# Two rows per partition, and a cut last group, in an average pool over windows of 16

## Chip, core and metric

One core of one Trainium2 chip runs the kernel; the other cores are idle. The metric is the device time of one execution in microseconds (us). The profile's span is 1.7 to 2.2 us shorter than that time in the runs here. All runs were single-core runs with a granted clock of 1.0, agreeing within 0.3%. A ratio below is the mean time of one kernel's runs over that of the other's runs of the same rounds, so it is not quite the ratio of the medians that stand beside it.

## The reference

The input is 32 x 256 rows of 4096 float32. Every row is cut into 256 windows of 16 neighbours, and the output is the mean of each window.

```python
x = np.random.randn(32, 256, 4096).astype(np.float32)     # 134 MB in
for i in range(256):
    result[:, :, i] = np.mean(x[:, :, 16 * i : 16 * (i + 1)], axis=-1)   # 8.4 MB out
```

There is one addition per loaded number, so the kernel is a stream: load, sum, scale, store.

## The kernel before

The 8192 rows go in 64 blocks of 128, one row to a partition. SyncE issues a 2 MB load, VectorE sums each window, ScalarE multiplies by 1/16, and ScalarE's queue issues a 128 KB store.

```python
xpool = ctx.enter_context(tc.tile_pool(name="xpool", bufs=8))
opool = ctx.enter_context(tc.tile_pool(name="opool", bufs=8))
for i in range(ntiles):                      # 64
    r0 = i * P
    x_tile = xpool.tile([P, length], mybir.dt.float32)
    nc.sync.dma_start(out=x_tile, in_=x_flat[r0 : r0 + P, :])
    o_tile = opool.tile([P, output_size], mybir.dt.float32)
    nc.vector.reduce_sum(out=o_tile,
        in_=x_tile.rearrange("p (o w) -> p o w", w=window), axis=mybir.AxisListType.X)
    nc.scalar.mul(out=o_tile, in_=o_tile, mul=inv_w)
    nc.scalar.dma_start(out=out_flat[r0 : r0 + P, :], in_=o_tile)
```

## Time and profile before

| | before |
|---|---|
| time, median | 345.66 us (345.62 to 345.74, 4 runs) |
| span of the profiled run | 343.8 us |
| VectorE busy | 282.9 us, 82% |
| bytes moved, mean rate | 142.65 MB, 415 GB/s |
| last load packet ends (DMA packet records) | 335.84 us |
| from there to the end of the span | 8.0 us |

These are lines of the page of the kernel before: VectorE's (DVE) share, the span in 40 slices (DMA is the mean busy share of the 16 DMA engines in tenths), the DMA queues (q1 carries the loads, q10 the stores), the group of reduces, and the DMA issues with the median time from issue to landing.

```profile
DVE 282.9 (82%) x64; ACT 28.0 (8%) x65; POOL 0.2 (0%) x4
...
DMA  8999999999999999999999999999999999999991
GB/s 305 427 423 435 432 427 423 425 434 431 427 421 424 437 428 425 425 424 439 428 423 425 427 435 425 427 423 431 434 427 423 423 429 435 427 425 422 434 419 39
DMA packets 18436, 142.65 MB, mean 415 GB/s; under 512 B 2048, under 2 KB 10240, under 8 KB 10240
...
q1 hardware_dynamic: 9216, 134.22, 91.4%
q10 hardware_dynamic: 9216, 8.39, 7.0%
...
L47 DVE TENSOR_REDUCE o_tile<-x_tile 128x256 f32<-128x4096 f32 x64 | 282.9, 4420 | 57.9 <-DMA x_tile<-in_x_dram 57.9
...
x_tile<-in_x_dram SPq DMA_DIRECT2D x64, 2048.0 KB, 20.8
out_dram<-o_tile ACTq DMA_DIRECT2D x64, 128.0 KB, 10.1
```

The DMA row is full from the second slice to the second-last, and VectorE's idle time is all spent waiting for loads: the DMA engines are the limit. VectorE is not far behind, though: 4.42 us of work for each block, against about 5.2 us between landings.

The end of the chain that ended last (start us, duration us, what):

```profile
315.45 20.77 DMA x_tile<-in_x_dram
...
336.35 4.43 DVE o_tile L47
340.78 0.02 issue
340.80 0.42 ACT o_tile L52
```

The last block's reduce, multiply and store come after all loading is done. That tail of 8 us has the DMA engines nearly idle (mean busy share 0.10 to 0.11 from 336 us on).

The trace also has a record of each DMA packet. Sorted by size, the median durations in both kernels (the rows from 2 KB on in the second column are from the changed kernel) are:

```
 4 B semaphore write    9 ns     2 KB store packet    84 ns
 1 KB store packet     46 ns    16 KB load packet    611 ns
 352 B store packet    21 ns    32 KB load packet   1213 ns
```

They fit 8.4 ns per packet plus 0.0368 ns per byte.

### The profile page before, as it was taken

What the parts mean: (1) busy time and instruction counts of PE and PEld (TensorE: products, weight loads), DVE (VectorE), ACT (ScalarE), POOL (GpSimd) and SP (SyncE); (2) the same over time, 40 slices, a digit from 0 to 9 for tenths busy, and PEclk for the clock granted to TensorE, in tenths of its full rate; (3) what the DMA queues carried; (4) which work ended last, traced back from release to release, by engine and by line L of the source; (5) the groups of instructions that cost most, each with busy time, mean ns of one, the idle gap of its engine ahead of it and who ended that gap; (6) DMA issues with size and microseconds to landing.
All of it is one profiled execution on the core that took longest, in us unless ns stands there. A gap on an engine that the chain in (4) does not pass through costs nothing.

```text
span 343.8 us, 475 instructions
## 1 busy us (share of the span) xinstructions
DVE 282.9 (82%) x64; ACT 28.0 (8%) x65; POOL 0.2 (0%) x4
## 2 busy tenths in 40 slices
DVE  0988988988888889889888888888888888898895
ACT  1000000000000000000000000000000000000000
POOL 0000000000000000000000000000000000000000
DMA  8999999999999999999999999999999999999991
GB/s 305 427 423 435 432 427 423 425 434 431 427 421 424 437 428 425 425 424 439 428 423 425 427 435 425 427 423 431 434 427 423 423 429 435 427 425 422 434 419 39
DMA packets 18436, 142.65 MB, mean 415 GB/s; under 512 B 2048, under 2 KB 10240, under 8 KB 10240
## 3 DMA queue, kind: packets, MB, share of 16 engines
q1 hardware_dynamic: 9216, 134.22, 91.4%
q10 hardware_dynamic: 9216, 8.39, 7.0%
q14 instruction: 4, 0.03, 0.0%
HBM read 134.22 MB, written 8.39 MB: 415 GB/s over the span
## 4 chain that ended last, share of the span: by engine, by line
DMA 97%; DVE 1%; SPq 0%; issue 0%; ACT 0%; DVEq 0%
DMA x_tile<-in_x_dram 97%; DVE o_tile L47 1%; SPq L44 0%; ACT o_tile L52 0%; DVEq L47 0%
## 5 line engine op out<-in xcount | busy, mean ns | idle before, releaser
L47 DVE TENSOR_REDUCE o_tile<-x_tile 128x256 f32<-128x4096 f32 x64 | 282.9, 4420 | 57.9 <-DMA x_tile<-in_x_dram 57.9
L52 ACT ACTIVATE o_tile<-o_tile 128x256 f32<-128x256 f32 x64 | 26.7, 417 | 312.5 <-DVE o_tile L47 312.5
L52 ACT ACT_TABLE_LOAD x1 | 1.3, 1283 | 0.7 <-PEq L70 0.7
L70 POOL MEMSET const-bfloat16-1.0<- 128x1 bf16 x1 | 0.1, 102 | 0.0
L70 POOL MEMSET const-uint8-127<- 128x1 uint8 x1 | 0.1, 102 | 0.0
L70 POOL MEMSET const-float32-0.0<- 128x1 f32 x1 | 0.1, 99 | 0.2 <-issue 0.2
L70 POOL MEMSET const-float32-1.0<- 128x1 f32 x1 | 0.1, 99 | 0.0
## 6 DMA issues: line engine op xcount, KB each, us to landing
x_tile<-in_x_dram SPq DMA_DIRECT2D x64, 2048.0 KB, 20.8
out_dram<-o_tile ACTq DMA_DIRECT2D x64, 128.0 KB, 10.1
```

The costliest lines, as they stand in the source:

```text
L47: nc.vector.reduce_sum(out=o_tile, in_=x_tile.rearrange("p (o w) -> p o w", w=window), axis=mybir.AxisListType.X,)
L52: nc.scalar.mul(out=o_tile, in_=o_tile, mul=inv_w)
L70: nc = _bacc.Bacc("TRN2", target_bir_lowering=False, num_devices=1)
```

## The change

Two things are intended: larger transfers for 7/8 of the rows (two neighbouring rows to a partition, so 4 MB loads in 32 KB pieces and 256 KB stores in 2 KB pieces), and a shorter tail (the last 1024 rows in pieces, the last one 1408 columns, with its multiply on VectorE). Cut to its core:

```diff
-    xpool = ctx.enter_context(tc.tile_pool(name="xpool", bufs=8))
-    opool = ctx.enter_context(tc.tile_pool(name="opool", bufs=8))
-    for i in range(ntiles):
-        ... (the loop above)
+    xbig, xmed, xsml: 3 buffers each; oacc: 8; osml: 4
+    x_p = x_flat[0:nb].rearrange("(n p r) l -> n p r l", p=P, r=2)   # nb = 7168 rows
+    o_p = o_flat[0:nb].rearrange("(n p r) o -> n p r o", p=P, r=2)
+    for g in range(28):
+        acc = oacc.tile([P, 2, O], FP, tag="acc", name="acc")
+        xt = xbig.tile([P, 2, L], FP, tag="x2", name="xt")
+        nc.sync.dma_start(out=xt, in_=x_p[g])
+        nc.vector.reduce_sum(out=acc, in_=xt.rearrange("p r (o w) -> p r o w", w=w), axis=AX)
+        nc.scalar.mul(out=accf, in_=accf, mul=inv_w)        # accf: acc, flat
+        nc.scalar.dma_start(out=o_p[g], in_=acc)
+    # last 1024 rows: 8 neighbouring rows to a partition, block r = row r of each partition
+    LB = [[384, 3712], [640, 3456], [896, 3200], [1280, 2816],
+          [1536, 2560], [1792, 2304], [2048, 2048], [1024, 1664, 1408]]
+    for r in range(8):
+        for c in LB[r]:
+            load x_g[:, r, c0:c0+c] into the next small (8 KB) or middle (16 KB) buffer
+            nc.vector.reduce_sum(...)                       # into ob_t[:, o0:o1]
+            if r == 7: multiply this piece (VectorE for the last, else ScalarE), store it
+        if r < 7: nc.scalar.mul(ob_t), nc.scalar.dma_start(o_g[:, r, :], ob_t)
```

## The prediction

> **What bounds the kernel now.** The DMA engines. The 40-slice rows show DMA at 9 in every slice but the first and last, at 421 to 439 GB/s; the chain of waits gives 97% to "DMA x_tile<-in_x_dram". VectorE is busy 82%: 64 reduces of 4.42 us, each waiting only for its load. The end of the chain: the last load lands at 336.25 us, then the reduce (4.43), ScalarE's multiply (0.42), the store's issue at 341.25, the end at 343.8. So 336 us are transfer and 7.6 us a serial tail.
>
> **What a transfer costs.** In the trace's DMA packet records a 16 KB load packet takes 611 ns, a 1 KB store packet 46, a 4-byte semaphore write 9. Two points give 0.0368 ns per byte and 8.4 ns per packet. [...] Per engine, up to the last load: 512 x 0.613 + 504 x 0.046 + semaphores 1.1 = 338 us of packets in 334 us of time.
>
> **What the change does there.** 7/8 of the rows go two to a partition: 32 KB load packets (estimate 1213 ns instead of 2 x 611) and 2 KB store packets (84 instead of 92), with half the semaphore writes. Per engine: loads -2.0 us, stores -1.8, semaphores -0.4. The last 1024 rows go in 17 smaller loads and 10 stores: +0.7. Sum -3.5 us, all on the critical path: the last load lands near 332.7 us.
>
> **The tail.** Intended: the last reduce has 1408 instead of 4096 columns, 1.5 us. But the last 4 MB reduce takes 8.84 us, and VectorE enters the last 1024 rows that far behind. Those rows take the DMA about 43 us and VectorE 8 x 4.42 plus about 1 for nine more instructions: 8.8 + 36.4 = 45.3. So it finishes some 2.3 us after the last landing, not 1.5. Then a VectorE multiply (0.2) for ScalarE's 0.42, and the same 2.6 us from store issue to end. Tail: 5.2 instead of 7.6 us: -2.4.
>
> **Order and buffers.** With three 4 MB buffers a load is issued when the reduce three back ends, with about 11 us of transfer still queued (estimate): the queue stays fed. [...] (eight 1 KB packets per engine spread over 5.1 us beside loads), so stores should land near 18 to 20 us instead of 10.1. In the last rows some loads wait for a store two or three blocks back through a shared semaphore; I expect bubbles of a microsecond at most, hidden by VectorE's backlog.
>
> **Prediction.** 345.7 - 3.5 - 2.4 = 339.8 us, 80% range 337.8 to 343.0. Faster by over 2%: 0.16; within 2%: 0.80; slower: 0.04.
>
> **What would show each step.** DMA packets near 11,950 instead of 18,436; mean GB/s up by 1%; last landing at 332 to 333 us; a chain ending with several reduces back to back and 4.5 to 5.5 us after that landing; VectorE still busy about 283 us.
>
> **What would make it wrong.** 32 KB rows split into smaller packets (-2 us of the gain). The last rows, 128 KB apart and in pieces of 1.5 to 15 KB, being slower to read: GB/s falling in the last 45 us. Loads there waiting longer for stores: idle DMA. The 352-byte store being slow.

## The result, and the profile after

The changed kernel takes 340.90 us (340.75 to 341.04, 8 runs) against 345.68 (345.39 to 345.93, 12 runs) for the kernel before: ratio 0.9862, 95% interval 0.9852 to 0.9872. It is faster by 1.4%, within 2%. The predicted gain was 5.9 us, the measured one 4.8.

The same lines of the page of the changed kernel, with both groups of reduces:

```profile
DVE 278.8 (82%) x46; ACT 22.4 (7%) x38; POOL 0.2 (0%) x4
...
DMA  8999999999999999999999999999999999999994
...
DMA packets 11955, 142.64 MB, mean 421 GB/s; under 512 B 1712, under 2 KB 2736, under 8 KB 7344
...
q1 hardware_dynamic: 6480, 134.22, 92.2%
q10 hardware_dynamic: 5472, 8.39, 6.6%
...
L77 DVE TENSOR_REDUCE acc<-xt 128x512 f32<-128x8192 f32 x28 | 243.2, 8686 | 56.8 <-DMA xt<-in_x_dram 56.8
L117 DVE TENSOR_REDUCE ob_t<-xt 128x128 f32<-128x2048 f32 (+15 forms) x17 | 35.5, 2154 | 1.0 <-DMA xt<-in_x_dram 0.7
...
xt<-in_x_dram SPq DMA_DIRECT2D x28, 4096.0 KB, 22.2
out_dram<-acc ACTq DMA_DIRECT2D x28, 256.0 KB, 14.9
```

A third of the packets are gone, and the mean rate went from 415 to 421 GB/s. A reduce of 8192 columns takes 8686 ns, less than twice 4420. The difference of the two, 4266 ns for 4096 columns, is 0.96 columns per ns, and leaves 154 ns as the fixed part of a reduce. By these two numbers a reduce of 2048 columns takes 2.29 us, and 2.29 us is what the trace of the changed kernel shows.

VectorE's instructions in order of time at the end of the changed kernel (start us, us, instruction; in brackets its idle time just before and what ended it; several back to back are merged):

```profile
291.29 8.69 DVE L77 TENSOR_REDUCE acc<-xt 128x512 f32<-128x8192 f32 x1 [1.68 <-DMA xt<-in_x_dram]
299.89 26.40 DVE L117 TENSOR_REDUCE ob_t<-xt 128x24 f32<-128x384 f32 x12
326.61 2.29 DVE L117 TENSOR_REDUCE ob_t<-xt 128x128 f32<-128x2048 f32 x1 [0.32 <-issue]
329.32 3.41 DVE L117 TENSOR_REDUCE ob_t<-xt 128x128 f32<-128x2048 f32 x2 [0.43 <-DMA xt<-in_x_dram]
332.96 3.41 DVE L117 TENSOR_REDUCE ob_t<-xt 128x104 f32<-128x1664 f32 x2 [0.23 <-DMA xt<-in_x_dram]
336.41 0.20 DVE L122 TENSOR_SCALAR ob_t<-ob_t 128x88 f32<-128x88 f32 x1
```

From the landing of the last 4 MB load at 291.3 us on, VectorE works for 45 us with 1 us of pauses. It works off the backlog of the big reduce only 10 us before the end.

The last load packet ends at 334.17 us instead of 335.84: the transfer part gained 1.7 us of the 3.5 predicted. From there to the end of the span are 5.0 us instead of 8.0: the tail gained 2.9 instead of 2.4.

Did the loads of the last rows stall on stores? The packet records say no. Their count of packets in flight falls below the number of engines for 0.03 us (mean over the engines) between 291 and 332 us, although SyncE spent 22.5 us of that time waiting for stores; enough loads were always queued. (It is a count over all engines, so a short pause of one could hide behind an overlap on another.) So the missing 1.8 us is hardly idle DMA.

### The profile page after: what moved, and what is told of

It is laid out like the page before. It is cut to its first block, busy times and chain, and to the rows that moved or that the text cites. A ratio compares the mean times of both kernels' runs of the same rounds, so it can differ in the third digit from the quotient of the medians.

```text
span 339.2 us, 311 instructions
## 1 busy us (share of the span) xinstructions
DVE 278.8 (82%) x46; ACT 22.4 (7%) x38; POOL 0.2 (0%) x4
## 4 chain that ended last, share of the span: by engine, by line
DMA 71%; DVE 28%; ACT 0%; issue 0%; DVEq 0%; SPq 0%
DMA xt<-in_x_dram 67%; DVE acc L77 26%; DMA out_dram<-acc 2%; DMA out_dram<-ob_t 2%; DVE ob_t L117 2%; ACT acc L81 0%; ACT ob_t L129 0%; DVEq L77 0%; DVE ob_t L122 0%; SPq L115 0%
## 5 line engine op out<-in xcount | busy, mean ns | idle before, releaser
L77 DVE TENSOR_REDUCE acc<-xt 128x512 f32<-128x8192 f32 x28 | 243.2, 8686 | 56.8 <-DMA xt<-in_x_dram 56.8
L117 DVE TENSOR_REDUCE ob_t<-xt 128x128 f32<-128x2048 f32 (+15 forms) x17 | 35.5, 2154 | 1.0 <-DMA xt<-in_x_dram 0.7
L81 ACT ACTIVATE acc<-acc 128x512 f32<-128x512 f32 x28 | 17.6, 629 | 281.0 <-DVE acc L77 281.0
L129 ACT ACTIVATE ob_t<-ob_t 128x256 f32<-128x256 f32 x7 | 2.9, 417 | 28.5 <-DVE ob_t L117 28.5
## 6 DMA issues: line engine op xcount, KB each, us to landing
out_dram<-acc ACTq DMA_DIRECT2D x28, 256.0 KB, 14.9
```

The costliest lines, as they stand in the source:

```text
L77: nc.vector.reduce_sum(out=acc, in_=xt.rearrange("p r (o w) -> p r o w", w=w), axis=AX)
L81: nc.scalar.mul(out=accf, in_=accf, mul=inv_w)
L117: nc.vector.reduce_sum(out=ov, in_=xv.rearrange("p (o w) -> p o w", w=w), axis=AX)
L129: nc.scalar.mul(out=ob_t, in_=ob_t, mul=inv_w)
```

## The experiments

The records suggest where it went. Summed per engine, load and store packets last longer than the time that passes: with 16 engines, the kernel before has 16.20 packets in flight on average between 40 and 280 us, the changed kernel 16.10. Between them the two queues overlap by 3.07 us before and 1.55 us after; per store packet that is about 8.3 ns in each (the overlap of semaphore writes counted in), the size of the fixed cost itself. So the two theories of the transfer part were:

- **O (overlap):** while loads and stores alternate, the store packet's 8.4 ns hide behind the load. Only fewer load packets pay.
- **P (packets):** every packet's 8.4 ns is paid, and the loss lies in the last rows.

### 1. Load and store packet size, each alone

Four kernels with the same instructions: 28 pairs of blocks with 4 MB loads and 256 KB stores, then the last eight blocks as in the kernel before (2 MB loads, no pieces). A pad between the two rows of a tile in SBUF splits its packets: with the x tile padded a load goes in 16 KB packets, with the accumulator padded a store goes in 1 KB packets (packets in all: 10369 without pads, 13953 with either, 17537 with both).

```diff
-        acc = oacc.tile([P, 2, O], FP, ...)
-        xt = xbig.tile([P, 2, L], FP, ...)
+        acc = oacc.tile([P, 2, O + OPAD], FP, ...)[:, :, :O]     # OPAD = 0 or 16
+        xt = xbig.tile([P, 2, L + XPAD], FP, ...)[:, :, :L]      # XPAD = 0 or 16
...
-    (last 1024 rows in pieces)
+    for i in range(56, 64): (the loop of the kernel before)
```

Load 32 KB, store 2 KB (no pads):

> Two rows per partition in 7/8 of the rows (32 KB load packets, 2 KB store packets), the last 1024 rows exactly as in the kernel before (2 MB loads, 4096-column last reduce). The transfer part of the change alone. Theory O (the packet records of a load and a store that alternate overlap by 8.4 ns, so the 8.4 ns per packet is paid once per load-store pair, not once per packet): -1.9 us from packets and -0.4 from semaphore writes, 343.4 us. Theory P (every packet's 8.4 ns is paid; the loss of the other 1.7 us lies in the last rows of the changed kernel): -3.8 and -0.4, 341.5 us. The overlap of packet records should be half of before's.

Load 16 KB, store 1 KB (both padded), the control:

> Control of the set of four: the same loads of 4 MB and stores of 256 KB, but the tiles in SBUF are padded between the two rows, so that a load goes in 16 KB packets and a store in 1 KB packets, as before. Both theories: only half the semaphore writes, 345.3 us, within 0.3 of before.

Load 16 KB, store 2 KB:

> Loads in 16 KB packets, stores in 2 KB packets. Theory O: 16 load packets per 8 store packets; each store packet saved was hidden beside a load anyway, so halving their number saves nothing: 345.3 us. Theory P: 3584 fewer store packets of 8.4 ns on 16 engines, -1.9 against the control: 343.4 us.

Load 32 KB, store 1 KB:

> Loads in 32 KB packets, stores in 1 KB packets: 16 store packets per engine against 8 load packets. If the engine alternates strictly between its two queues, one packet each, stores get through at half the rate at which they are made; they pile up until the eight accumulators are full (about pair 16), then the reduce and with it the loads wait for stores: slower than the control, my guess 350 us, with the median time of a store from issue to landing at 60 us or more. If an engine takes several store packets in a turn, there is no pile, and Theory O gives 343.4 (all the packet gain is the loads'), Theory P 343.4 as well.

Measured, against 345.72 us (345.62 to 346.11) for the kernel before in the same rounds. The last column is the time from the moment at which 5 MB of loads and stores had been moved to that at which 120 MB had, by the packet records (each packet's bytes spread evenly over its duration). It is free of the start and the end of the kernel. For the kernel before it is 268.84 us, and traces of kernels that are alike up to there agree in it within 0.01 us.

| load packets | store packets | median us | ratio, 95% interval | last load packet ends | in flight, 40 to 280 us | 5 to 120 MB, us |
|---|---|---|---|---|---|---|
| 16 KB | 1 KB | 344.62 | 0.9967, 0.9955 to 0.9980 | 334.75 | 16.20 | 268.38 |
| 16 KB | 2 KB | 344.63 | 0.9970, 0.9957 to 0.9982 | 334.64 | 16.15 | 267.82 |
| 32 KB | 2 KB | 342.65 | 0.9907, 0.9892 to 0.9922 | 332.73 | 16.10 | 266.48 |
| 32 KB | 1 KB | 347.88 | 1.0059, 1.0046 to 1.0071 | 338.17 | 16.04 | 269.00 |

Beside 16 KB loads, larger store packets gained nothing in time; beside 2 KB stores, larger load packets gained 1.98 us. That is close to what 8.4 ns for each of 3584 packets over 16 engines come to (1.9), but in part by chance: in both runs with a padded x tile the first load packet starts at 2.15 us, in all others at 1.72 to 1.76, so some 0.4 us of the 1.98 is a later start that the pad brought with it.

The last column is free of that. In its stretch, 8.4 ns for every packet saved would come to 1.73 us for the loads and as much for the stores (an estimate: 1.88 us, times 115 of the 124.8 MB that go in pairs). Measured are 1.34 us for the loads (267.82 to 266.48) and 0.56 us for the stores (268.38 to 267.82): about three quarters and one third. So P, which expects both in full, falls. O as I wrote it is not exact either: store packets were not quite free, and the overlap did not halve between the first two rows. The rates from 40 to 280 us show the same (the control, then 2 KB stores, then 32 KB loads as well; columns: stretch, its length, VectorE's, ScalarE's and GpSimd's busy time, clock, DMA share, GB/s):

```profile
40.00:280.00 240.00, 200.61 (x24) 14.48 (x23) 0.00 (x0) 1.00 1.01 428
```
```profile
40.00:280.00 240.00, 200.72 (x24) 14.47 (x23) 0.00 (x0) 1.00 1.01 429
```
```profile
40.00:280.00 240.00, 201.41 (x24) 15.10 (x24) 0.00 (x0) 1.00 1.01 431
```

What the 2 KB stores gained in rate was gone at the end: 2 KB stores were served sooner (10.4 us from issue to landing against 15.8), so less of them was left for after the last load, where stores run beside the last reduce (packet records: 293 KB against 452 KB).

The control missed its expectation: 1.1 us faster than the kernel before instead of 0.4. It has 896 fewer semaphore writes, 56 per engine of 9 ns each, 0.46 us in the stretch from 5 to 120 MB, and 0.46 us is what it gains there (268.84 to 268.38). So the semaphore writes were worth what I had put them at. The rest of its gain lies at the end. There its stores lag more, so that 1.3 us of store packets per engine run after the last load instead of 0.8; that this is the cause is argued from the records, not shown by a run.

The last row is the one in which a smaller store did harm. Its waits (engine, line, what it waited for: us in total, times, longest) and its store issues:

```profile
ACT acc L50 <- DMA out_dram<-acc: 108.0, 8, 18.2
...
DVE acc L47 <- DMA out_dram<-acc: 17.8, 2, 10.1
```
```profile
out_dram<-acc ACTq DMA_DIRECT2D x28, 256.0 KB, 32.7
```

With 16 store packets against 8 load packets per engine, stores fall behind, until, some 150 us into the kernel, reduces wait for accumulators that are still being stored. The direction was expected; the size was not (347.9 instead of my guess of 350, 32.7 us instead of 60 to landing), because stores catch up while the loads stand still (from 184 to 188 us no load packet starts, and stores move at 269 GB/s). The time to landing goes with the number of store packets for each load packet: with 16 KB loads and 2 KB stores, half as many store as load packets, a store landed in 10.4 us, with equal numbers in 14.9 to 15.8, with twice as many in 32.7. And in the kernel before, the eight 1 KB packets that a store has on each engine are spread over 5.0 us (packet records, median of the 64 stores), the time of about eight load packets of 0.61 us. Both fit two queues that take turns packet by packet; that the engines work so is inferred from these numbers. So in the change, merging stores is not worth time by itself, but larger loads need it.

Pairs with 2 KB stores and uncut last rows let the last load packet end at 332.73 us; the changed kernel's ends at 334.17. So with the last rows in pieces (and eight to a partition) the last load packet ends 1.4 us later; the prediction had 0.7. But the pieces themselves cost less: the moments at which 141.8 of the 142.6 MB had been moved, 331.44 and 332.01 us, are only 0.6 us apart. Most of the rest is stores that the changed kernel serves before its last load and not after it, where they run beside the last reduces: 0.39 us of store packets per engine are left there instead of 0.87.

### 2. What the pieces at the end are worth

One run is the kernel before with only its last block cut in three; one has pairs, seven uncut blocks and a last block cut in three.

```diff
-    for i in range(64):
+    for i in range(63):                      # pairs_cut: 28 pairs, then range(56, 63)
         (the loop of the kernel before)
+    for c in [1024, 1664, 1408]:             # columns of block 63
+        load, reduce, multiply (VectorE for the last), store
```

Last block alone cut, nothing else changed:

> The kernel before with only its last block of 128 rows cut in columns of 1024, 1664 and 1408, the last multiply on VectorE: the tail part of the change alone. Here VectorE has no backlog (each reduce is shorter than the time between landings), so the tail after the last landing should be 1.5 to 1.8 us of reduce instead of 4.43, -2.7, and 0.2 saved on the multiply; two more loads and stores cost 0.2 to 0.3: 342.9 us.

Pairs, and only the last block cut:

> Pairs of rows in 7/8 of the rows, then seven uncut blocks of 128 rows (2 MB loads in 16 KB packets, 1 KB stores) and only the last block cut in three. It tells what cutting the other seven blocks in two is worth. Theory O with the cost of the cuts as the two traces show it (from the landing of 7/8 of the bytes to the last load packet 42.0 us uncut, 43.6 cut): faster than the changed kernel by about 1.0 to 1.3, 339.8 us. The rival, that the cuts pay by feeding VectorE in smaller pieces while it works off its backlog: slower than the changed kernel, 341.5 or more.

The first measured 344.77 us (ratio 0.9974, 0.9962 to 0.9987), a gain of 0.9 us where 2.8 was expected. The second measured 341.79 (0.9888, 0.9875 to 0.9902), slower than the changed kernel where I expected it faster; the rival was right. Both misses have one main cause. VectorE at the end of the first:

```profile
331.24 4.42 DVE L43 TENSOR_REDUCE o_tile<-x_tile 128x256 f32<-128x4096 f32 x1 [0.78 <-DMA x_tile<-in_x_dram]
335.58 4.53 DVE L57 TENSOR_REDUCE ob_t<-xc 128x64 f32<-128x1024 f32 x3
340.14 0.21 DVE L61 TENSOR_SCALAR ob_t<-ob_t 128x88 f32<-128x88 f32 x1
```

and of the second:

```profile
327.80 4.42 DVE L60 TENSOR_REDUCE o_tile<-x_tile 128x256 f32<-128x4096 f32 x1 [0.78 <-DMA x_tile<-in_x_dram]
332.13 4.53 DVE L74 TENSOR_REDUCE ob_t<-xc 128x64 f32<-128x1024 f32 x3
336.69 0.20 DVE L78 TENSOR_SCALAR ob_t<-ob_t 128x88 f32<-128x88 f32 x1
```

While the three pieces land, VectorE is still summing the whole block in front of them. The end is set by that block's landing plus 8.9 us of reduces, however finely the last block is cut. In the kernel before the last reduce ended at 340.78, now at 340.1: the cut gained only the pause that VectorE used to make. A block in hand is a backlog too. The changed kernel's falling pieces (3712, 3456, ..., 2048, then 1664, 1408) shorten it step by step: its last reduce ends at 336.4 us although its last load packet ends at 334.2; in the run without the earlier cuts it ends at 336.7 with the last load packet at 333.2. That is 0.3 of the 0.7 us between the two spans (339.2 and 339.9); the other 0.4 lies after the last store packet (1.8 us to the end of the span instead of 1.4) and is not explained.

### 3. Stores out of the way of the loads, and the backlog

The tail has idle DMA engines (share 0.07 from 334 to 336 us in the changed kernel, 0.11 from 336 us on). So the results of the last eight blocks were kept in one tile and stored late. The runs differ in where the pairs end (block 56, as in the change, or 48, followed by eight single blocks) and in whether the last eight blocks are in pieces.

```diff
+    acc8 = opool.tile([P, 8, O], FP, ...)
+    for r in range(8):
+        for c in ([4096] if r < 7 else [1024, 1664, 1408]):
+            load; reduce into acc8[:, r, ...]; multiply
+        if r == 6: nc.scalar.dma_start(out=o_g[:, 0:7, :], in_=acc8[:, 0:7, :])
+        if r == 7 and second-last piece: store the first 168 columns of row 7
+    # the last 88 columns: VectorE multiply, stored through SyncE's queue
```

Uncut blocks, pairs up to block 56, then up to block 48:

> As pairs_cut, but the last 1024 rows go eight to a partition, and the results of seven of the eight last blocks go out in one store when all seven are done, about when the last load lands, in the time in which the DMA engines would otherwise be idle; the very last store goes through the other queue. If loads and stores share one saturated resource, about 2.3 us of store packets move behind the last load, which then lands about 2 us earlier. But VectorE then enters these rows 8.7 us behind and gains only about 0.45 us a block: it should end some 4 us after the last landing with its last reduces back to back, so that most of the gain is lost: 339.0 us.

> As late28, but pairs only up to block 48, then eight single blocks with their own stores in which VectorE works off the backlog of the last pair (about 0.75 us a block), then the last eight as in late28. Costs 0.4 us in packets and semaphore writes. If the backlog is what holds late28 back, this ends 1.5 to 2.5 us after its last landing and beats it: 337.8 us. If late28 is not held back by VectorE, it is slower than late28 by 0.4.

They measured 341.16 us (ratio 0.9870, 0.9856 to 0.9883) and 341.08 (0.9865, 0.9850 to 0.9881), neither faster than the changed kernel, where 339.0 and 337.8 us were expected. The transfer did as expected: the last load packet ended at 331.82 and 332.16 us, 2 us before the changed kernel's. But VectorE's last reduce ended at 336.2 and 336.5, again 8.9 us after the landing of the seventh block, which had an uncut block and three pieces to sum. I had blamed the backlog of the last pair; removing it (the run with pairs up to block 48) changed nothing. VectorE waits for each of its last blocks there, and works without a pause only from the seventh on:

```profile
322.73 4.42 DVE L78 TENSOR_REDUCE acc<-xc 128x256 f32<-128x4096 f32 x1 [0.48 <-DMA xc<-in_x_dram]
327.64 8.86 DVE L78 TENSOR_REDUCE acc<-xc 128x256 f32<-128x4096 f32 x4 [0.49 <-DMA xc<-in_x_dram]
```

The uncut block in front was the limit.

So the pieces of the changed kernel came back, with late stores. All results but the last 88 columns go out in one store after the second-last piece:

```diff
-        for c in ([4096] if r < 7 else [1024, 1664, 1408]):
+        for c in LB[r]:                      # the pieces of the changed kernel
...
-        if r == 6: store rows 0 to 6
+        if r == 7 and second-last piece: store rows 0 to 6 and the first 168 columns of row 7
```

> Three things together: pairs only up to block 48 and eight single blocks (VectorE works off the backlog of the last pair), the last eight blocks in the pieces of the changed kernel, and one late store for their results, issued after the second-last multiply, so that nearly no store packet is served beside the last loads. Theory V (the end is the later of two bounds: the last landing plus its reduce, and for every earlier landing that landing plus all VectorE work after it): last load packet near 331.7 us, both bounds near 333.6, end of the span near 336.4, time 338.1 us, faster than before by over 2%. Rival T (only the transfer counts, VectorE's backlog doesn't matter): same as tap28_late within 0.4.

> As tap24_late, but pairs up to block 56 as in the changed kernel. Theory V: VectorE enters the last rows 8.7 us behind at about 291.2 us and needs 8.7 + 36 us without a pause, so its last reduce ends at 335.9 whenever the loads land; no idle time of VectorE in the last 40 us; time 340.3 us, 2 us slower than tap24_late. Rival T: 338 us, with the last landing 2 us earlier than in the changed kernel deciding.

> As tap24_late, but each of the last blocks has its own store, as in the changed kernel. The last load lands no earlier than in the changed kernel (four pairs fewer cost 0.4 us), so less backlog alone buys nothing: 340.8 us, within 0.4 of the changed kernel. If the backlog alone were what cost time in the changed kernel: 339.5 or less.

Measured, against 345.72 us (345.59 to 345.91) in the same rounds:

| pairs up to | stores of the last blocks | median us | ratio, 95% interval | last load packet | last reduce ends |
|---|---|---|---|---|---|
| block 48 | late | 340.57 | 0.9851, 0.9834 to 0.9867 | 332.52 | 334.8 |
| block 56 | late | 341.13 | 0.9867, 0.9852 to 0.9882 | 332.36 | 334.9 |
| block 48 | own | 341.17 | 0.9867, 0.9853 to 0.9882 | 334.55 | 336.7 |
| block 56 (the changed kernel, other rounds) | own | 340.90 | 0.9862, 0.9852 to 0.9872 | 334.17 | 336.4 |

The third row came as expected: less backlog alone buys nothing. The first two were to be 2 us apart by my theory, within 0.4 if VectorE's backlog did not matter, and are 0.6 apart: neither was right. With pairs up to block 56 and late stores VectorE indeed works without a pause to the end:

```profile
291.07 8.69 DVE L50 TENSOR_REDUCE acc<-xt 128x512 f32<-128x8192 f32 x1 [1.62 <-DMA xt<-in_x_dram]
299.67 35.23 DVE L98 TENSOR_REDUCE a<-xc 128x24 f32<-128x384 f32 x17
334.94 0.21 DVE L102 TENSOR_SCALAR a<-a 128x88 f32<-128x88 f32 x1
```

It is the floor that I had put at 335.9 us, at 334.9. But the run with eight single blocks ends its reduces at 334.8 too, with short waits before its larger pieces: for it the limit is a landing 6.7 us of reduces earlier.

```profile
328.02 6.73 DVE L98 TENSOR_REDUCE a<-xc 128x128 f32<-128x2048 f32 x4 [0.20 <-DMA xc<-in_x_dram]
```
And in both the reduces end 1.5 us before the changed kernel's, of which little or nothing arrives in the time. The stretches of the first run (pairs up to block 48) show why (VectorE, ScalarE, GpSimd, clock, DMA share, GB/s):

```profile
330.00:332.00 2.00, 2.00 (x3) 0.56 (x2) 0.00 (x0) 1.00 0.82 338
332.00:334.00 2.00, 2.00 (x2) 0.29 (x1) 0.00 (x0) 1.00 0.01 6
334.00:336.00 2.00, 0.96 (x2) 0.00 (x0) 0.00 (x0) 1.00 0.84 345
336.00:338.00 2.00, 0.00 (x0) 0.00 (x0) 0.00 (x0) 1.00 0.48 179
```

The DMA engines are idle from 332 to 334 us, and then the late store is itself the tail. The last run moves only that store: rows 0 to 6 go out as soon as they are multiplied.

```diff
-        if r == 7 and second-last piece: store rows 0 to 6 and the first 168 columns of row 7
+        if r == 6 and last piece:        store rows 0 to 6
+        if r == 7 and second-last piece: store the first 168 columns of row 7
```

> As tap24_late, but seven of the eight last blocks go out in one store as soon as the seventh is multiplied, not after the second-last piece of the eighth. In tap24_late the DMA engines stood idle from 332 to 334 us and the late store then ran from 334 to 337 us beside the very last one, whose span ended 3.7 us after the last multiply (2.55 in the changed kernel). If the late store's position is what holds it back: packets from 331.7 us on, the very last store's 2.55 us after its multiply, end of the span near 337.6, time 339.4 us. If the end is set otherwise: as tap24_late, 340.6 us.

It measured 339.66 us (339.34 to 339.71, 5 runs) against 345.76 (345.67 to 346.17): ratio 0.9821, 0.9807 to 0.9834, where 339.4 us was expected. Its stretches:

```profile
330.00:332.00 2.00, 2.00 (x3) 0.57 (x2) 0.00 (x0) 1.00 1.03 422
332.00:334.00 2.00, 2.00 (x2) 0.29 (x1) 0.00 (x0) 1.00 0.90 378
334.00:336.00 2.00, 0.82 (x2) 0.00 (x0) 0.00 (x0) 1.00 0.26 80
336.00:338.00 2.00, 0.00 (x0) 0.00 (x0) 0.00 (x0) 1.00 0.00 0
```

The store now fills the hole, and only the last 88 columns are left for the end. This version beats both kernels: the changed kernel's ratio to the kernel before is 0.9862, and the two intervals do not touch. (Its interval just meets that of the one late store, 0.9834 to 0.9867; the single runs, at most 339.71 and at least 340.39, do not.) Whether it needs the eight single blocks is not shown: the two stores were not tried with pairs up to block 56, where the reduces end only 0.3 us later.

## Why the prediction was right, point by point

It put the time at 339.8 us with a range of 337.8 to 343.0, and within 2% at 0.80. It measured 340.9, 1.4% faster. That the sum came within 1.1 us is partly luck: one term, the stores, was too large by over a microsecond, the range was wide enough for it, and the tail came out shorter than predicted. In its terms:

- **The DMA engines bound the kernel: right.** All of VectorE's idle time was waiting for loads, and the packet records show hardly an idle moment until the last load.
- **Loads, -2.0 us: right, but too large.** Doubling the load packets alone measured -1.98, of which some 0.4 is the padded runs' later start; from 5 to 120 MB, 1.34 of 1.73 us were gained.
- **Stores, -1.8 us: wrong.** Doubling the store packets alone measured 0.0 in time, and 0.56 of 1.73 us from 5 to 120 MB. The step that failed is reading a packet's recorded duration as time that is paid in full: the records of the two queues overlapped, by about the fixed cost of a store packet in the kernel before.
- **Semaphore writes, -0.4: right.** The control, which has half the DMAs and the old packet sizes, gained 0.46 us from 5 to 120 MB. In time it gained 1.1; the rest lies at the end, and stores that run after the last load are the likely cause.
- **Last rows in pieces, +0.7: right for the pieces,** 0.6 us at 141.8 MB moved. The last load packet ended 1.4 us later than with uncut last rows, because more of the stores had been served before it.
- **Sum of the transfer, -3.5: measured -1.7** at the last load packet, and -2.2 at the moment at which 141.8 MB had been moved (334.21 to 332.01 us). The store term is most of the error, the load term a part, and stores served before the last load the rest.
- **The tail, -2.4: measured -2.9.** The backlog that the prediction counted was real: from the landing of the last pair to the end of the last reduce VectorE took 45.1 us, nearly without a pause, where 45.3 were predicted.
- **Stores landing near 18 to 20 us: 14.9.** Later than before (10.1), less than expected.
- **Bubbles of a microsecond at most from loads waiting for stores: right,** 0.03 us.
- Packets near 11,950: 11,955. Last landing at 332 to 333 us: too early, the last packet ended at 334.2. VectorE busy about 283 us: 278.8, as a double reduce takes less than two.

Left open: the part of the control's gain that lies at the end, why two thirds of a store packet's fixed cost but only a quarter of a load packet's did not count, and the 0.4 us at the end of the run with pairs and one cut block.

## What to carry to other kernels

A packet's recorded duration need not be its price: here, with loads and stores on two queues, halving the number of store packets gained 0.56 of an estimated 1.73 us. Before counting on a saving, halve the number of those packets alone and time it, and look whether the test itself shifts the start or the end. When the loads here got larger packets and the stores did not, the stores fell behind (32.7 us to landing, 347.88 us instead of 342.65): make the store packets larger too. In a stream whose compute takes 85% of the transfer time, as here, cutting the last piece alone gained little (0.9 us where 2.8 was expected), because the pieces before it did not shrink too: the end is the latest, over all landings, of that landing plus all the work still to be done after it, here 8.9 us of reduces after the landing of the block in front. Here it paid to hold the stores of the last blocks back until the loads were nearly done (issued at 330.6 us, last load packet at 332.4), and then to issue them at once, into the time in which the last reduces leave the DMA engines idle (share from 332 to 334 us: 0.01 with the one late store, 0.90 with it issued in two).
